# A planner's durations from the trace, values centred before the recurrence, subtractions moved to POOL, and a third lane in one hybrid layer

## The chip, the core and the metric

The kernel runs on one core of a Trainium2 chip. The metric is the device time of one execution in microseconds (us), as the median of three runs. TensorE is PE in what follows, its weight loads are PEld, VectorE is DVE, ScalarE is ACT, GpSimd is POOL and SyncE, which issues most DMAs, is SP.

## The reference

One layer of a diffusion backbone works on 1024 latent tokens behind 256 context tokens, with 1024 channels, all in float32. The parts that matter here:

```python
def wkv7_scan(r, decay, k, v, a, b, s0, reverse):
    # S_t = S_(t-1) diag(w_t) + (S_(t-1) a_t) b_t^T + v_t k_t^T ; y_t = S_t r_t
...
    for d in range(N_DIR):                       # forward and backward
        ys_c, s_ctx = wkv7_scan(*ins_c, s_zero, rev)
        ys_l, _ = wkv7_scan(*ins_l, s_ctx, rev)
        wkv_l = wkv_l + ys_l
        bonus_l = bonus_l + bon_l

def readout(wkv, bonus, gd):                     # per head of 64 channels
    mu = jnp.mean(wkv, -1, keepdims=True)
    var = jnp.mean(jnp.square(wkv - mu), -1, keepdims=True)
    yn = ((wkv - mu) * lax.rsqrt(var + LNX_EPS)).reshape(...)
    yn = yn * p['rwkv_lnx_g'] + p['rwkv_lnx_b']
    g = jax.nn.sigmoid(gd) @ p['rwkv_g_up']
    return ((yn + bonus.reshape(yn.shape)) * g) @ p['rwkv_w_out']
```

Around it stand an input projection, an S5 branch, gates, an output projection and a convolutional feed-forward network. The output of the recurrence is linear in `v`, so taking the mean over a head's 64 channels off `v` takes it off the output `wkv`; the bonus uses `v` with its mean.

## The kernel before

The kernel has three stages. **Stage A** makes the input projection and the S5 branch and writes the operands of the recurrence to DRAM. For each of the eight pairs of heads, `rw_job` leaves `xs` (the values), 80 PE transposes in all (L683) turn it by 128x128 pieces into PSUM tiles `pvt`, ACT copies them to `vt`, and DMAs store `vT_d`.

**Stage B** is the recurrence, for eight pairs of heads one after the other, 20 chunks of 64 tokens each. A *preparation* (`prep_nodes`) makes the operands of four chunks in one direction in a *lane* of buffers; there are two lanes, taken in turn. `inverse_nodes` inverts the small triangular blocks of up to eight chunks: DMAs L to LD to LN, 30 small DVE operations (L1073, L1076), DMAs TN to TD and TT to AD to AT, then small matmuls. `chain_nodes` is the recurrence itself, one step for each chunk: PE makes X, ACT copies X, PE makes U, DVE copies U (L1244), PE makes the new state, DVE writes S (L1267), and so on. `final_nodes` is the readout, in four blocks of 256 tokens a pair: loads of `y_d`, a DVE sum (L1336), a PE matmul by `E.center`, which takes the mean off (L1330), ACT scale and square, PE sums, 12 small DVE operations (L155 to L163), two spreads on PE, and more DVE work; it uses one buffer `fin`, and in the last pair three free blocks named `Q` as well. Beside all this runs the *filling*: gate and S5 matmuls that depend on nothing in the recurrence, 512 groups of three matmuls of 512 columns (L1464 to L1466). Their float32 operands are split in a high and a low half by `split`: SP loads `fr`, ACT makes the high half `fwh` or `fxh` (L1443), DVE subtracts it for the low half `fwl` or `fxl` (L1444).

The order of PE, ACT and DVE in stage B is written out by a *planner* (`Plan.order`). Each node has an engine, a cost in us and dependencies; the planner plays the engines through with these costs and emits the nodes in the order of its play. On PE a filling group is taken when little was issued lately or nothing else is ready. POOL and SP follow the emitted program through the framework's own scheduler.

**Stage C** holds the output projections and the feed-forward network; its first matmul (L202, `ygh`) needs `yg_d`, which the readout stores.

Of the kernel before, what the change touches and what calls it, by code (L numbers as in the profile page):

```python
# [12 lines left out]
AF = mybir.ActivationFunctionType  # L13
# [582 lines left out]
def stage_a(E):  # L596
    nc = E.nc
    with ExitStack() as st:
# [73 lines left out]
        for j in range(8):  # L672
# [48 lines left out]
class Node:  # L721

    __slots__ = ("eng", "cost", "deps", "succ", "emit", "due", "take", "give", "left", "ready", "bank", "cols", "fill", "tag", "key", "pri", "second")

    def __init__(self, eng, cost, deps, emit):
# [3 lines left out]
        self.cols, self.fill, self.tag, self.key, self.second = 0.0, None, None, False, None  # L729
# [7 lines left out]
class Plan:  # L737
# [19 lines left out]
    def order(self):  # L757
# [43 lines left out]
        def pick(h):  # L801

            skip, best = [], None
# [14 lines left out]
        while True:  # L818
# [8 lines left out]
            for e in heaps:  # L827
# [9 lines left out]
                if h or (e == "p" and fills):  # L837
# [6 lines left out]
                    else:  # L844
# [4 lines left out]
                        best = best or pick(h)  # L849
# [12 lines left out]
            n = best  # L862
            if n.eng == "p":
                hot.append((now, n.cols))
                total += n.cols
                left -= n.fill is None
# [6 lines left out]
            end = now + n.cost  # L873
# [30 lines left out]
def prep_nodes(E, g, c0, d, k):  # L904
# [37 lines left out]
    zn.cols = 2048  # L942
# [7 lines left out]
    for half in range(2):  # L950
# [6 lines left out]
        th.append(op("a", 0.36, [zn, ms], tanh, give=zs[half]))  # L957
    ts_ = op("v", 0.2, [th[0]], lambda: nc.vector.tensor_scalar(P[:, :, 1:65], P[:, :, 1:65], 0.5, 0.5, op0=OP.mult,
                                                                op1=OP.add))
    flat = P.rearrange("p c t -> p (c t)")  # L960
    scan = op("v", 0.34, [ts_], lambda: nc.vector.tensor_tensor_scan(flat, E.m65, flat, 0.0, op0=OP.mult, op1=OP.add))
    epi = op("a", 0.4, [scan], lambda: nc.scalar.activation(PI, P[:, :, 1:65], AF.Exp, scale=KAP,
                                                             bias=E.ln_half))
    ep = op("a", 0.31, [epi], lambda: nc.scalar.activation(P, P, AF.Exp, scale=-KAP))
    pc = op("g", 0.1, [ep], lambda: nc.gpsimd.tensor_copy(g.PC.tile[:, d, c0:c0 + nb], P[:, :, 64]))
    q = [op("v", 0.4, [ep, lkk], lambda: nc.vector.scalar_tensor_tensor(
        Q[:, :, 0:64], v3(o_(kk)), -1.0, P[:, :, 0:64], op0=OP.mult, op1=OP.mult))]
    t1 = op("v", 0.34, [th[1]] + q, lambda: nc.vector.scalar_tensor_tensor(kk, o_(ta), 1.0, kk, op0=OP.add,
                                                                           op1=OP.mult))
    tid = op("g", 0.54, [t1], lambda: nc.gpsimd.tensor_scalar(ta, ta, E.par("ka", j), E.ka2[:, j:j + 1], op0=OP.mult,  # L970
                                                              op1=OP.add))
    tk = op("v", 0.34, [tid, lkx], lambda: nc.vector.tensor_mul(ta, ta, o_(kx)))
    bk = [op("v", 0.4, [t1, epi], lambda: nc.vector.tensor_mul(BK[:, :, 0:64], v3(o_(kk)), PI))]
    bkk = op("v", 0.4, [tk, epi], lambda: nc.vector.tensor_mul(BK[:, :, 64:128], v3(ta), PI))
    rq = []
    if lat:
        rq = [op("v", 0.4, [ep, lr], lambda: nc.vector.tensor_mul(Q[:, :, 64:128], v3(o_(r)), P[:, :, 1:65]))]
        rkh = E.half[:, 32 + 8 * d + j:33 + 8 * d + j]
        bon = op("v", 0.4, [tk] + rq, lambda: nc.vector.scalar_tensor_tensor(r, o_(ta), rkh, r, op0=OP.mult,
                                                                              op1=OP.mult))  # L980
        g.done.append(op("g", 1.0, [bon], lambda: nc.gpsimd.dma_start(E.bon_d[j, d, :, bs], r)))
# [3 lines left out]
    for h in range(2):  # L985
        w = op("p", (0.5 if lat else 0.4), sc[-1:] or bk + [bkk] + q + rq, None, take=None if h else "F")
# [12 lines left out]
        w.emit, w.cols = mm, 8 * nn  # L999
# [13 lines left out]
    mq = [op("g", 1.2 if lat else 0.7, [cp], lambda: nc.gpsimd.tensor_mul(  # L1013
        A[:, :, 0:nn], A[:, :, 0:nn], E.mask[:, None, 0:nn].to_broadcast([128, 4, nn])))]
    tp = op("p", 0.35, bk + [bkk, blk.gate], None, take="F")
# [11 lines left out]
    tp.emit = tr  # L1027
# [882 lines left out]
```

## Time and profile before

| | |
|---|---|
| median of 3 runs | 3253.95 us (3245.26 to 3255.84) |
| profiled execution, its own time | 3263.26 us |
| span of the profile | 3261.5 us |
| mean granted PE clock | 0.913 of full |
| PE busy share of the span | 89% |
| DVE, ACT, POOL busy share | 56%, 42%, 14% |

The span is the time from the first to the last instruction; the execution's own time is 1.8 us longer, and 9.3 us above the median. A granted clock of 1.00 is 2.4 GHz, 0.50 is 1.2 GHz; a value between says that a stretch held both.

### The profile page before, as it was taken

What the parts mean: (1) busy time and instruction counts of PE and PEld (TensorE: products, weight loads), DVE (VectorE), ACT (ScalarE), POOL (GpSimd) and SP (SyncE); (2) the same over time, 40 slices, a digit from 0 to 9 for tenths busy, and PEclk for the clock granted to TensorE, in tenths of its full rate; (3) what the DMA queues carried; (4) which work ended last, traced back from release to release, by engine and by line L of the source; (5) the groups of instructions that cost most, each with busy time, mean ns of one, the idle gap of its engine ahead of it and who ended that gap; (6) DMA issues with size and microseconds to landing.
All of it is one profiled execution on the core that took longest, in us unless ns stands there. A gap on an engine that the chain in (4) does not pass through costs nothing.

```text
span 3261.5 us, 83856 instructions
## 1 busy us (share of the span) xinstructions
PE 2911.9 (89%) x34806; PEld 2197.0 (67%) x34806; DVE 1838.5 (56%) x4640; ACT 1371.0 (42%) x3055; POOL 471.7 (14%) x781
## 2 busy tenths in 40 slices
PE   6999887878579898999889888899998999999998
PEld 1788676767446666666666666666775888887876
DVE  7668777663345454668575667655534444344343
ACT  5224544435235454555444555442314433333332
POOL 0430011011222222223131222211000000000000
PEclk8999898989789888889788998889998999999999
DMA  5663333333465565455555455544531111113332
GB/s 190 207 168 104 128 117 125 110 119 120 145 167 148 152 161 135 120 135 133 130 143 126 119 141 146 125 125 139 193 120 55 52 48 49 46 52 112 107 107 74
DMA packets 556879, 399.32 MB, mean 122 GB/s; under 512 B 374225, under 2 KB 460497, under 8 KB 555217
## 3 DMA queue, kind: packets, MB, share of 16 engines
q1 hardware_dynamic: 517824, 300.96, 33.5%
q0 software_dynamic: 29312, 87.75, 8.0%
q10 hardware_dynamic: 9360, 5.25, 0.8%
q8 instruction: 273, 4.47, 0.6%
q14 instruction: 110, 0.89, 0.1%
HBM read 286.16 MB, written 112.85 MB: 122 GB/s over the span
## 4 chain that ended last, share of the span: by engine, by line
PE 61%; DMA 11%; issue 9%; DVE 9%; ACT 5%; SPq 3%; POOL 1%; ACTq 0%; DVEq 0%; POOLq 0%
PE pd L202 8%; PE pd L203 8%; PE pd L204 8%; PE bank L1464 5%; PE bank L1465 3%; PE bank L1466 3%; PE bank L1189 3%; PE bank L1184 3%; PE o L1751 3%; PE o L1752 3%; PE o L1753 2%; DMA wraw<-win 2%; PE bank L1330 1%; PE bank L994 1%; PE bank L947 1%
## 5 line engine op out<-in xcount | busy, mean ns | idle before, releaser
L189 DVE TENSOR_TENSOR wlo<-wraw,whi 128x512 fp32r<-128x512 f32 x276 | 184.0, 689 | 493.6 <-ACT whi L188 492.9
L188 ACT ACTIVATE whi<-wraw 128x512 fp32r<-128x512 f32 x276 | 165.8, 627 | 490.8 <-PE pd L203 243.4
L202 PE MATMUL pd<-hh,whi 128*128 128x512 f32 (+1 forms) x744 | 285.8, 384 | 51.8 <-ACT xs L624 35.2
L1464 PE MATMUL bank<-fxh,fwh 128*128 128x512 f32 x512 | 277.4, 542 | 12.1 <-ACT fo L1487 8.6
L202 PE MATMUL pd<-h2h,whi 128*128 128x512 f32 x704 | 275.5, 392 | 12.3 <-ACT h2h L1639 12.2
L204 PE MATMUL pd<-hh,wlo 128*128 128x512 f32 (+1 forms) x744 | 280.9, 378 | 1.5 <-DVE wlo L189 1.5
L203 PE MATMUL pd<-hl,whi 128*128 128x512 f32 (+1 forms) x744 | 282.1, 379 | 0.0
L204 PE MATMUL pd<-h2h,wlo 128*128 128x512 f32 x704 | 278.9, 397 | 0.0
L203 PE MATMUL pd<-h2l,whi 128*128 128x512 f32 x704 | 278.3, 396 | 0.3 <-DVE h2l L1640 0.2
L1465 PE MATMUL bank<-fxl,fwh 128*128 128x512 f32 x512 | 221.2, 432 | 0.5 <-issue 0.5
L1466 PE MATMUL bank<-fxh,fwl 128*128 128x512 f32 x512 | 220.8, 431 | 0.0
L202 PEld LDWEIGHTS pd<-hh,whi 128*128 128x128 f32 x744 | 148.3, 199 | 81.6 <-ACT xs L624 38.3
L204 PEld LDWEIGHTS pd<-hh,wlo 128*128 128x128 f32 x744 | 147.7, 199 | 25.8 <-DVE wlo L189 2.0
L203 PEld LDWEIGHTS pd<-hl,whi 128*128 128x128 f32 x744 | 148.4, 199 | 23.8 <-issue 2.5
L202 PEld LDWEIGHTS pd<-h2h,whi 128*128 128x128 f32 x704 | 133.2, 189 | 45.7 <-ACT h2h L1639 15.6
L203 PEld LDWEIGHTS pd<-h2l,whi 128*128 128x128 f32 x704 | 133.2, 189 | 33.0 <-DVE h2l L1640 2.1
L204 PEld LDWEIGHTS pd<-h2h,wlo 128*128 128x128 f32 x704 | 133.6, 190 | 26.6
L1464 PEld LDWEIGHTS bank<-fxh,fwh 128*128 128x128 f32 x512 | 104.3, 204 | 62.0 <-issue 20.0
L1444 DVE SCALAR_TENSOR_TENSOR fwl<-fr,fwh 128x512 fp32r<-128x512 f32 x128 | 92.6, 724 | 86.9 <-ACT fwh L1443 86.3
L1073 DVE TENSOR_TENSOR PR<-TN,LN 128x1 f32<-128x1 f32 (+9 forms) x360 | 118.5, 329 | 39.8 <-DMA LN<-LD 35.6
L1751 PE MATMUL o<-ph,whi 128*128 128x512 f32 x352 | 137.8, 396 | 2.2 <-ACT p L1725 2.2
L1752 PE MATMUL o<-pl,whi 128*128 128x512 f32 x352 | 138.9, 395 | 0.0
(395 smaller groups left out, 7209.3 us busy)
## 6 DMA issues: line engine op xcount, KB each, us to landing
wraw<-up SPq DMA_DIRECT2D x88, 256.0 KB
wraw<-down SPq DMA_DIRECT2D x88, 256.0 KB
wraw<-win SPq DMA_DIRECT2D x68, 256.0 KB
fin<-wmod SPq DMA_DIRECT2D x32, 512.0 KB
fr<-win SPq DMA_DIRECT2D x64, 256.0 KB
fr<-glu SPq DMA_DIRECT2D x64, 256.0 KB
s5U<-u_d SPq DMA_DIRECT2D x32, 320.0 KB
kk<-kk_d SPq DMA_DIRECT2D x80, 128.0 KB
```

The lines of the kernel that those rows point to most:

```text
L188: nc.scalar.activation(hi[:, c], raw, AF.Copy)
L189: nc.vector.tensor_sub(lo[:, c], raw, hi[:, c])
L202: nc.tensor.matmul(pt[:, :n], hi[:, c], xh, start=k == 0, stop=False)
L203: nc.tensor.matmul(pt[:, :n], hi[:, c], xl, start=False, stop=False)
L204: nc.tensor.matmul(pt[:, :n], lo[:, c], xh, start=False, stop=k == 7)
L1073: last = [op("v", 0.07 + k * k / 960.0, last, lambda lo=lo, hi=hi, k=k, s=s: nc.vector.tensor_tensor(out=PR[al, :k * k].rearrange("l (c m) ...
L1184: nc.tensor.matmul(out[OWN[e], d], w[OWN[e]], x[OWN[e]], skip_group_check=True, tile_position=(64 * e, 64 * e), **kw)
L1464: nc.tensor.matmul(o, hi[:, c], xh[:, k, :], start=k == 0, stop=False)
L1465: nc.tensor.matmul(o, hi[:, c], xl[:, k, :], start=False, stop=False)
L1466: nc.tensor.matmul(o, lo[:, c], xh[:, k, :], start=False, stop=k == 7)
L1751: nc.tensor.matmul(o, hi[:, c], ph, start=k == 0, stop=False)
L1752: nc.tensor.matmul(o, hi[:, c], pl, start=False, stop=False)
```

## The change

- The planner's costs are set to durations of the trace (the scan from 0.34 to 0.69 us, the readout's small operations from 0.07 to 0.2, chain matmuls from 0.35 to 0.23, and so on). A node carries a `mode`, the array shape of its matmuls: the planner adds 0.1 us where the shape changes, and prefers a node of the same shape within 0.5 us of due time. The counts of columns of two kinds of nodes change.
- The values are multiplied by `E.center` (identity minus the head's mean) in stage A, by 80 plain matmuls where 80 transposes stood. The 32 `center` matmuls of the readout and one ACT operation for each are gone; the scale joins a DVE operation.
- `split` subtracts on POOL where the scale is 1 (144 of 160 subtractions: the 128 weights and half of the 32 operands).
- Three lanes instead of two; the ring of value buffers `V` has two instead of three.

```diff
-                    nc.tensor.transpose(pv[:, q, :], xs[:, 128 * (i + q):128 * (i + q) + 128], E.ident)
+                    nc.tensor.matmul(pv[:, q, :], xs[:, 128 * (i + q):128 * (i + q) + 128], E.center, start=True, stop=True)
...
+            if mode is not None:
+                ok = [x for x in h if x[2].take is None or len(self.free[x[2].take]) > (x[2].second is not None)]
+                if not ok:
+                    return None
+                x = min(ok, key=lambda x: (x[0] + AFFINE * (x[2].mode != mode), x[1]))
...
-                        best = best or pick(h)
+                        best = best or pick(h, last)
...
+                shape, last = SWITCH * (n.mode != last), n.mode
...
-    scan = op("v", 0.34, [ts_], lambda: nc.vector.tensor_tensor_scan(flat, E.m65, flat, 0.0, op0=OP.mult, op1=OP.add))
+    scan = op("v", 0.69, [ts_], lambda: nc.vector.tensor_tensor_scan(flat, E.m65, flat, 0.0, op0=OP.mult, op1=OP.add))
...
-        pc = mm(E.center, Y, [a])
-        a = op("a", 0.27, [pc], lambda Y=Y, pc=pc: nc.scalar.activation(Y, E.ps(pc)[:, 0:256], AF.Copy, scale=E.par("lg", j)), give=pc)
-        q = op("a", 0.27, [pc], lambda y1=y1, pc=pc: nc.scalar.activation(y1, E.ps(pc)[:, 0:256], AF.Square), give=pc)
+        q = op("a", 0.38, [a], lambda Y=Y, y1=y1: nc.scalar.activation(y1, Y, AF.Square))
...
-LANES, PERIOD, SLACK, EVAC, STRETCH = 2, 120.0, 3.0, 0.0, 2.0
+LANES, PERIOD, SLACK, EVAC, STRETCH = 3, 120.0, 3.0, 0.0, 2.0
...
-        l = add("v", 0.6, [h], lambda: nc.vector.scalar_tensor_tensor(lo, r, scale, hi, op0=OP.mult, op1=OP.subtract))
+        if scale == 1.0:
+            l = add("g", 1.33, [h], lambda: nc.gpsimd.tensor_sub(lo, r, hi))
+        else:
+            l = add("v", 0.7, [h], lambda: nc.vector.scalar_tensor_tensor(lo, r, scale, hi, op0=OP.mult, op1=OP.subtract))
...
-        E.V = Ring(pl, [tile_(p, [128, 2, 4, 64], f"V{k}") for k in range(3)])
+        E.V = Ring(pl, [tile_(p, [128, 2, 4, 64], f"V{k}") for k in range(2)])
```

PE at the end of the recurrence, before (the last chain matmuls are those on `RB` and on `Q,S`; `fwh` and `fwl` are the filling):

```order
L1464 MATMUL bank_7321<-fxh,fwh_7431 128x512
L1465 MATMUL bank_7321<-fxl,fwh_7431 128x512
L1466 MATMUL bank_7321<-fxh,fwl_7434 128x512
L1330 MATMUL bank_7317<-fin_7422,center 128x256
L1184 MATMUL bank_7320<-RB_7417,U_7349 64x64 x4
L1184 MATMUL bank_7320<-Q_7415,S_7354 64x64 x4
L1330 MATMUL bank_7316<-fin_7422,bones 128x256
L1464 MATMUL bank_7321<-fxh,fwh_7429 128x512
L1465 MATMUL bank_7321<-fxl,fwh_7429 128x512
L1466 MATMUL bank_7321<-fxh,fwl_7432 128x512
L169 MATMUL bank_7315<-bones,fin_7422 128x2 x2
```

PE at the same place of the change (lines 1198 and 1203 are the chain, 1344 the readout, 1483 to 1485 the filling):

```order
L1485 MATMUL bank_7321<-fxh,fwl_7439 128x512
L1203 MATMUL bank_7320<-Q_7421,V_7393 64x64 x2
L1198 MATMUL bank_7319<-X_7348,TX_7341 64x64 x2
L1198 MATMUL bank_7320<-RB_7423,U_7349 64x64 x4
L1198 MATMUL bank_7320<-Q_7421,S_7354 64x64 x4
L169 MATMUL bank_7317<-bones,fin_7428 128x2 x2
L1344 MATMUL bank_7314<-fin_7428,bones 128x256
L176 MATMUL bank_7315<-ident,fin_7428 64x128 x4
L1344 MATMUL bank_7316<-fin_7428,gw_7429 128x256
L169 MATMUL bank_7317<-bones,Q_7403 128x2 x2
```

Before, 44 filling groups and six readout blocks stand behind the last chain matmul; in the change no filling group and five readout blocks do, and the `center` matmuls are gone.

POOL in the middle of stage B, before (L965 and L970 belong to a preparation, L1013 masks a block `Q`):

```order
L965 COPY PC_7359<-P_7373 128x4
L939 MEMSET P_7373 128x4
L970 TENSOR_SCALAR ta_7372<-ta_7372,par_t,ka_113 128x256
L1013 TENSOR_TENSOR Q_7397<-Q_7397,mask 128x4x64 x2
L1488 DMA sg_d<-fo_7436 1024x1x64
L1293 DMA y_d<-RB_7405 128x256 x2
L965 COPY PC_7359<-P_7366 128x4
```

And in the change (L1461 is the subtraction, L984 was L970, L1027 was L1013):

```order
L1461 TENSOR_TENSOR fwl_7438<-fr_7433,fwh_7435 128x512
L1027 TENSOR_TENSOR Q_7397<-Q_7397,mask 128x512
L1461 TENSOR_TENSOR fwl_7439<-fr_7434,fwh_7436 128x512
L1461 TENSOR_TENSOR fwl_7440<-fr_7432,fwh_7437 128x512
L979 COPY PC_7359<-P_7380 128x4
L953 MEMSET P_7380 128x4
L984 TENSOR_SCALAR ta_7379<-ta_7379,par_t,ka_113 128x256
L1027 TENSOR_TENSOR Q_7397<-Q_7397,mask 128x512
L1507 DMA sg_d<-fo_7442 1024x1x64
```

The subtractions stand between the masks and the preparations on POOL, in one queue with the stores of `y_d`, `sg_d` and `bon_d`.

## Rows read from the trace of the kernel before

**Rows 1.** The page, part 1: busy time, share of the span, instructions.

```profile
PE 2911.9 (89%) x34806; PEld 2197.0 (67%) x34806; DVE 1838.5 (56%) x4640; ACT 1371.0 (42%) x3055; POOL 471.7 (14%) x781
```

**Rows 2.** Windows: stretch, length, busy PE, PEld, DVE, ACT, POOL; clock, DMA share, GB/s.

```profile
640.00:885.00 245.00, 188.78 (x1149) 156.56 (x1148) 113.71 (x250) 100.51 (x168) 44.09 (x73) 0.87 0.44 136
920.00:2230.00 1310.00, 1178.78 (x25521) 829.31 (x25520) 804.68 (x2614) 639.98 (x1815) 313.43 (x499) 0.87 0.54 137
1000.00:1100.00 100.00, 92.97 (x2204) 64.30 (x2196) 58.78 (x184) 57.82 (x166) 27.41 (x44) 0.97 0.59 152
```

**Rows 3.** Windows of PE alone, around one stall: busy, granted clock.

```profile
1275.00:1280.00 5.00, 0.47 (x4) 0.66 0.69 105
1280.00:1285.00 5.00, 4.68 (x152) 0.50 0.80 261
...
1305.00:1310.00 5.00, 4.89 (x42) 0.50 0.35 101
1310.00:1315.00 5.00, 4.43 (x82) 0.93 0.33 46
```

**Rows 4.** Waits of PE, 920 to 2230: us in total, times, longest.

```profile
PE bank L1184 <- DVE U L1244: 21.3, 20, 3.2
PE bank L1330 <- DVE fin L1336: 19.1, 8, 6.4
PE bank L1109 <- DMA AT<-AD: 15.6, 14, 5.6
PE bank L1189 <- DVE S L1267: 10.0, 14, 3.6
```

**Rows 5.** Waits of SP's queue, 920 to 2230, same columns.

```profile
SPq L1442 <- DVE fwl L1444: 51.9, 16, 11.4
...
SPq L1442 <- DVE PR L1073: 34.3, 21, 6.2
```

**Rows 6.** Groups by line and form, 920 to 2230: busy, mean ns, idle before.

```profile
L1444 DVE SCALAR_TENSOR_TENSOR fwl<-fr,fwh 128x512 fp32r<-128x512 f32 x117 | 85.0, 728 | 79.3 <-ACT fwh L1443 78.8
...
L1013 POOL TENSOR_TENSOR Q<-Q,mask 128x512 f32<-128x512 f32 x62 | 82.0, 1328 | 71.6 <-ACT Q L1010 65.5 <-PE bank L1189 5.5
...
L961 DVE TENSOR_TENSOR_SCAN P<-m,P 128x260 f32<-128x260 f32 x76 | 52.8, 694 | 1.0
```

**Rows 7.** Line 683, whole run: duration min/median/max in ns.

```profile
L683 PE MATMUL pvt<-ident,xs x80: 272/273/477, 323.5 to 870.8; 128*128 128x128 f32 x80
```

**Rows 8.** Line 543, plain float32 matmuls of the same size, 64 instructions.

```profile
L543 PE MATMUL s5py<-s5U,s5M x128: 270/275/552, 295.6 to 785.9; 128*128 128x128 f32 x128
```

**Rows 9.** Timeline of PE: a `center` matmul between filling matmuls.

```profile
2247.40 0.59 PE L1330 MATMUL bank<-Q,center 128*128 128x256 f32 x2
...
2248.06 0.40 PE L1465 MATMUL bank<-fxl,fwh 128*128 128x512 f32 x1
```

**Rows 10.** Timeline: POOL and DVE at 1590 us.

```profile
1590.43 1.29 POOL L1013 TENSOR_TENSOR Q<-Q,mask 128x512 f32<-128x512 f32 x1
1590.50 1.25 DVE L161 SCALAR_TENSOR_TENSOR fin<-fin 128x4 f32<-128x4 f32 x1
```

**Rows 11.** Line 161, 920 to 2230: duration min/median/max in ns.

```profile
L161 DVE SCALAR_TENSOR_TENSOR fin<-fin x78: 147/161/1252, 1344.5 to 2218.3; 128x4 f32<-128x4 f32 x78
```

**Rows 12.** Timeline of PE and POOL from the recurrence's end to stage C.

```profile
2230.26 0.22 PE L1184 MATMUL bank<-Q,S 64*64 64x64 f32 x2
...
2261.66 0.54 POOL L1356 DMA_DIRECT2D yg_d<-fin  x1 [2.03 <-DVE fin L1354]
2276.90 0.54 POOL L1356 DMA_DIRECT2D yg_d<-fin  x1 [10.22 <-DVE fin L1354]
2278.89 0.39 PE L1464 MATMUL bank<-fxh,fwh 128*128 128x512 f32 x1
2279.57 0.39 PE L1464 MATMUL bank<-fxh,fwh 128*128 128x512 f32 x1
2287.19 0.80 PE L202 MATMUL pd<-ygh,whi 128*128 128x512 f32 x1 [6.77 <-ACT whi L188]
```

More of the change, by code (lines that the diff above doesn't have):

```diff
@@ L721 @@
 class Node:
-    __slots__ = ("eng", "cost", "deps", "succ", "emit", "due", "take", "give", "left", "ready", "bank", "cols", "fill", "tag", "key", "pri", "second")
+    __slots__ = ("eng", "cost", "deps", "succ", "emit", "due", "take", "give", "left", "ready", "bank", "cols", "fill", "tag", "key", "pri", "second", "mode")
     def __init__(self, eng, cost, deps, emit):
@@ L728, in __init__ @@
         self.succ, self.due, self.take, self.give, self.ready = [], 1e9, None, None, 0.0
-        self.cols, self.fill, self.tag, self.key, self.second = 0.0, None, None, False, None
+        self.cols, self.fill, self.tag, self.key, self.second, self.mode = 0.0, None, None, False, None, 128
 LAG = {"p": 0.27, "a": 0.22, "v": 0.22, "g": 0.25, "s": 2.2, None: 0.0}
@@ L799, in arrive, with pick @@
             heapq.heappush(wait[n.eng], (n.ready, seq[id(n)], n))
-        def pick(h):
+        last = 128
+        def pick(h, mode=None):
+            if mode is not None:
[3 more added lines that the diff above has]
+                x = min(ok, key=lambda x: (x[0] + AFFINE * (x[2].mode != mode), x[1]))
+                h.remove(x)
+                heapq.heapify(h)
+                return x[2]
             skip, best = [], None
@@ L862, in order @@
             n = best
+            shape = 0.0
             if n.eng == "p":
+                shape, last = SWITCH * (n.mode != last), n.mode
                 hot.append((now, n.cols))
@@ L872, in order @@
                 n.cost *= COLD
-            end = now + n.cost
+            end = now + n.cost + shape
             if n.eng == "p":
@@ L941, in prep_nodes @@
     zn = op("p", 0.44, gates, None, take="F")
-    zn.cols = 2048
+    zn.cols, zn.mode = 1024, 96
     zs = (zn, pl.second(zn))
@@ L998, in mm @@
                                      stop=True, tile_position=(64 * e, 64 - 64 * e))
-        w.emit, w.cols = mm, 8 * nn
+        w.emit, w.cols, w.mode = mm, 8 * nn, 64
     first = sc[0]
@@ L1240, in g2 @@
                 own(pU, d, tx[:, d, si, :], X.tile[:, d], start=end and d == 0, stop=True)
-        gu.emit, gu.cols = g2, 512
+        gu.emit, gu.cols, gu.mode = g2, 512, 64
         X.users.append(gu)
@@ L1292, in step @@
                 for d in HALF:
-                    g.done.append(op("g", 1.0, B.out, lambda d=d: nc.gpsimd.dma_start(
+                    g.done.append(op("g", 0.55, B.out, lambda d=d: nc.gpsimd.dma_start(
                         E.y_d[j, d, :, 64 * (i - 7):64 * (i - 3)], RB[:, d].rearrange("p c t -> p (c t)"))))
@@ L1458, in dense @@
                 k = 4 * half + q
-                n = add("p", 0.65, x[k] + parts, None, take=None if first else "D")
+                n = add("p", FILL, x[k] + parts, None, take=None if first else "D")
                 first = first or n
@@ L1486, in evac @@
                 out = E.sg_d[i, :, t0:t0 + 512]
-            n = add("a", 0.48, [last, g], lambda: nc.scalar.activation(dst, src(), AF.Tanh, scale=0.5), give=first)
-            o.users = [add("g", 1.0, [n], lambda: nc.gpsimd.dma_start(out, mem))]
+            n = add("a", 0.78, [last, g], lambda: nc.scalar.activation(dst, src(), AF.Tanh, scale=0.5), give=first)
+            o.users = [add("g", 0.6, [n], lambda: nc.gpsimd.dma_start(out, mem))]
             written[i, t0] = o.users[0]
@@ L1496, in evac_b @@
             sb, g = outs.next()
-            n = add("a", 0.48, [last, g], lambda: nc.scalar.activation(sb.tile, E.ps(first), AF.Tanh), give=first)
+            n = add("a", 0.6, [last, g], lambda: nc.scalar.activation(sb.tile, E.ps(first), AF.Tanh), give=first)
             hold[0] = sb, n
```

108 lines of the change are left out of this document (56 added, 52 removed).

## The prediction

> **What bounds the kernel now.** I read the busy shares first: PE is busy 89% of the span, DVE 56%, ACT 42%, POOL 14% [rows 1]. Then I read the windows, because these shares mix three stages. The recurrence fills 920 to 2230, and there PE is busy 1178.8 of 1310 us, DVE 804.7, ACT 640.0, POOL 313.4 [rows 2]. The reader is to see that PE is the bound there, yet falls short in two ways. It stands idle for 1310 - 1178.8 = 131 us, and its mean granted clock is 0.87. With levels of 1.0 and 0.5 that is 26% of the time at half rate, and half of that time, about 170 us, is lost where PE streams. So 301 us of the 1310 are no work at full clock.
>
> The two losses hang together. At 1275 PE does almost nothing for 5 us; the granted clock falls to 0.50 and is back at 0.93 only in the slice that begins at 1310 [rows 3]. A stall of some 5 us so costs some 15 us more. The stretch 1000 to 1100 shows what the same code does without such stalls: PE busy 93.0%, clock 0.97 [rows 2], a loss of 7 + 3 = 10 us in 100 in place of 23.
>
> Third, the waits of PE. Of its 131 us idle, 21.3 wait for DVE's copy of U, 19.1 for the readout's first DVE sum L1336, 10.0 for DVE's S, 15.6 for the DMA AT<-AD of the inversion [rows 4]; what is left is spread over ACT and many small causes. SP's queue, finally, waits 51.9 us in L1442 for a DVE subtraction that has not yet freed a buffer, and 34.3 us in the same line behind L1073 [rows 5]. SP issues in order, so the loads of the inversion and the readout stand behind that wait. Late DVE work is thus the largest single cause, directly and through SP.
>
> **The change, part by part.**
>
> *Centre matmuls, -14.* The readout loses 32 `center` matmuls. From the start of one, 2247.40, to the second matmul of the next filling group, 2248.06, are 0.66 us [rows 9]; a filling matmul alone takes a third of the 0.68 us between two groups' starts, 0.23 [rows 12]. A `center` so costs 0.43, 32 of them 14 us of PE. The stall of 19.1 before it does not go with it: the next matmul on PE (L169 on the squares) needs the same loads. It only can shrink, which the last item holds.
>
> *Transposes to matmuls, +8.* In stage A 80 transposes, one record each of 0.273 [rows 7], become plain float32 matmuls, for which such a matmul of the same size shows two records of 0.275 [rows 8]. At the most that is 80 x 0.275 = 22 us, at the least nothing, since PE is busy only 188.8 of 245 us where most of them lie [rows 2]. I take 8: PE is nearer to full than to free there.
>
> *Filling moved into the recurrence, +30; a shorter tail, -15.* In the order of before 44 filling groups stand behind the last chain matmul, in the change none. At 0.68 each [rows 12] that is 30 us of PE work that now has to be done before the chain ends. The tail that they leave, 2230.3 to 2287.2, is 56.9 us. It does not go away: the readout's loads, sums and stores take their time with nothing to hide behind. In the change five readout blocks follow instead of six, so the fifth, whose store in before was issued at 2261.7, is the last. From the last store at 2276.9 to stage C's first matmul took 10.3 [rows 12]. So 2261.7 - 2230.3 + 10.3 = 41.7, 15 less than 56.9.
>
> *Subtractions on POOL, +12.* 144 subtractions of 0.728 leave DVE [rows 6]: 105 us, 8% of the stretch. On POOL nothing like them is in the trace; the nearest row is the two-input mask L1013 of the same 128x512 at 1.328 [rows 6]. That gives 191 us, so POOL would be busy 504 of 1310: hidden as a sum. The price is elsewhere. A DVE operation of 128x4, L161, takes 0.161 in the median but 1.252 at worst [rows 11], and one such case began inside a POOL mask and ended with it [rows 10]. So the mask holds DVE out. If half of the 144 meet a DVE operation and hold it for half their length, 144 x 0.5 x 0.66 = 48 us are added to DVE, less than the 105 taken off. DVE has idle time for it; I let a quarter, 12, reach PE. Bounds: 0, if no subtraction meets the chain, and 48, if all of it does.
> The Trainium skill says it more broadly (GPSIMD Engine Reference, Specifications): POOL's SBUF interfaces are shared with VectorE, which contends when an instruction has two SBUF inputs or a two-port mode. By it any of the 144 could take its full 1.33 from DVE, 191 us against 105 taken off. The one case in rows 10 agrees, the median in rows 11 says that it is rare; it is the third rival below.
>
> *Third lane, value ring of two: 0.* A preparation is more ahead, so PE finds one more kind of work. A value buffer serves a block of four steps, some 4 x 1310 / 160 = 33 us; with two, the next one's loads can be issued when the block before last is done, a block ahead of need. If SP is held there all the same, the loads behind it are late, which the last item's lower bound holds.
>
> *The durations, -100.* The planner's play had DVE too fast: its cost for the scan was 0.34, the trace says 0.694 [rows 6], and the small readout operations stood at 0.07 against 0.161 [rows 11]. Chain matmuls it had too slow (0.35, now 0.23). So PE came to the chain's matmuls before DVE had written U and S; that is what rows 4 show. The four waits above are 66 of 131 us, half. With true durations and 105 us less DVE work I let two thirds of that half go, and the clock with it in proportion: 301 x 0.5 x 0.67 = 100. Bounds: 0, if the play was not the cause, and 189, if all of the stretch ran as 1000 to 1100 did (1310 - 301 = 1009 of work; 1009 / 0.9 = 1121).
>
> That the shapes now cost the planner something is worth nothing here: counted in both orders, PE changes the array shape 1341 times in stage B before and 1386 times in the change. The preference does not do what it is for.
>
> **Sum.** -14 + 8 + 30 - 15 + 12 - 100 = -79. Against the profiled execution of 3263.3 this is 3184; the median of the runs is 9.3 lower, so 3254 - 79 = 3175.
>
> **The rivals.**
>
> *Stalls all but gone.* If the recurrence runs like its best stretch, the last item is -189 in place of -100, and the sum is -168: 3086. For it: POOL takes what SP waited for, and a stall avoided saves three times itself [rows 3]. Against it: AT<-AD and the readout's loads hang on DMA, whose lag in the planner is unchanged.
>
> *The change does not do what it says.* If PE's waits come from how the engines drift from any play, true durations change nothing. Then the last item is 0 and the rest stays, +21: 3275, slower. For it: the moved filling has to be paid and POOL is a new in-order queue whose subtractions stand behind waits for others. Against it: the waits in rows 4 are on the engine whose costs were furthest off.
>
> *POOL holds DVE.* If each subtraction holds DVE for the full 1.33, DVE gains 191 - 105 = 86 us of work; the chain's copies of U and S stand behind it in DVE's queue, the durations are wrong again, and no stall goes. With half of the 86 on PE, 43 in place of 12, and no recovery: 3254 + 21 + 31 = 3306. It decides from the point where a subtraction holds DVE longer than the 0.73 that it takes off. For it: rows 10. Against it: the median of rows 11, and POOL's mask has run 62 times in this stretch beside a DVE busy 61%.
>
> **How the numbers follow.** My forecast holds with a chance of 0.46, its own range 3120 to 3225. The first rival has 0.27 (3060 to 3120), the second 0.14 (3240 to 3300), the third 0.06 (3290 to 3330); 0.07 is left for a small gain, 3225 to 3250. Forecast, first rival and most of the small gain are faster by over 0.3%, which is 10 us and about what a measurement of this kernel can tell from no change: 0.77. Within 0.3% lie the rest of the small gain and the near end of the second rival: 0.09. Slower: 0.14. The range 3060 to 3262 leaves out the third rival and most of the second.
>
> **What would show it.** In the profile after, between the first chain step and the last: PE's waits for U, S and the readout's first sum below 25 us together (50.4 now), a mean clock of 0.91 or more, PE idle below 95 us. SP's waits for `fr` should be short, or be for POOL. In the tail no filling matmul, and some 42 us from the last chain matmul to stage C. DVE's small operations should still have a median near 0.16; a mean above 0.4 would show the third rival. Stage A should end within 10 us of where it did. I am wrong if the clock stays at 0.87 with the waits only moved to other lines, or if DVE's two-input operations grow beside POOL's subtractions.

## The result and the profile after

The change is slower by about half a per cent: 3264.99 us in the median of 20 runs (3251.08 to 3284.94) against 3250.53 for the kernel before in 20 runs, a ratio of 1.0055 with a 95% interval of 1.0036 to 1.0075. I had forecast 3175. What came is close to the second rival, "the change does not do what it says" (3275), but by two errors that cancel, as the section on the prediction shows.

The profiled execution of the change spans 3265.7 us, that of before 3261.5. The one of before ran 12.8 us over its median (3263.3 against 3250.5), so the two profiles lie closer together (4.5 us) than the medians do (14.5), and what is read from them below accounts for the smaller difference. Line numbers in the changed kernel are larger by 1 in stage A, by 14 in stage B up to the readout and by up to 19 behind it.

Page of the change, part 1, to lay beside [rows 1]:

```profile
PE 2913.4 (89%) x34822; PEld 2200.2 (67%) x34822; DVE 1817.6 (56%) x4496; ACT 1361.7 (42%) x3023; POOL 655.1 (20%) x925
```

144 subtractions left DVE, yet DVE's busy time fell by 20.9 us only. That is taken up with e2.

Windows of the change, columns as in [rows 2]: the two stretches of [rows 2], then the chain from its first copy of U to its last, then the tail to stage C's first matmul.

```profile
920.00:2230.00 1310.00, 1168.27 (x25279) 820.81 (x25279) 792.31 (x2474) 635.52 (x1783) 491.27 (x637) 0.88 0.56 142
1000.00:1100.00 100.00, 98.53 (x2170) 65.67 (x2173) 45.50 (x139) 56.94 (x159) 36.45 (x47) 0.96 0.61 153
1015.40:2255.50 1240.10, 1118.45 (x24575) 791.91 (x24575) 747.08 (x2386) 604.77 (x1722) 452.88 (x592) 0.89 0.55 138
2255.50:2293.90 38.40, 20.67 (x97) 13.14 (x97) 20.74 (x99) 5.07 (x10) 4.30 (x8) 0.58 0.39 132
```

The same two stretches, chain and tail, in the kernel before:

```profile
979.00:2229.20 1250.20, 1124.81 (x24652) 796.46 (x24643) 769.00 (x2508) 612.73 (x1753) 296.92 (x475) 0.87 0.54 136
2229.20:2287.20 58.00, 48.06 (x259) 36.22 (x257) 33.97 (x130) 14.50 (x29) 5.95 (x11) 0.97 0.47 153
```

Three things are to be seen. The chain starts 36.4 us later (1015.4 against 979.0). It is 10.1 shorter, but not because PE stands still less: 1240.1 - 1118.5 = 122 us of it are idle, before 125. And the tail is 19.6 shorter, as 44 filling groups have left it. So stage C begins 36.4 - 10.1 - 19.6 = 6.7 us later.

Waits of PE in the change, 920 to 2230, to lay beside [rows 4]:

```profile
PE bank L1389 <- DMA fin<-wmod: 29.1, 6, 15.0
PE bank L1123 <- DMA AT<-AD: 25.2, 26, 4.8
PE bank L1198 <- DVE U L1258: 16.7, 19, 2.5
PE bank L1203 <- DVE S L1281: 10.5, 10, 1.9
...
PE bank L1344 <- ACT fin L1351: 5.1, 2, 2.8
PE bank L1344 <- DVE fin L1352: 5.0, 2, 2.8
```

The wait for the readout's first sum has gone with the `center` matmul; waits of 5.1 us for the readout's squares (L1351) and 5.0 for its sum of the bonus (L1352) are left in its place. U and S still hold PE for 27.2 us (31.3 before), and what the readout gave back is taken by two DMA waits: AT<-AD (15.6 before) and fin<-wmod, of which 10.1 lie in the chain (5.0 before) and 19.0 ahead of it, where the kernel before waits 14.9.

Waits of SP's queue in the same stretch, to lay beside [rows 5], and then SP's queue as stage B starts (start, length, operation):

```profile
SPq L1458 <- POOL fwl L1461: 102.9, 46, 9.8
```

```profile
907.60 15.48 SPq L1458 DMA_DIRECT2D fr<-xn_d  x1
...
938.64 2.10 SPq L1079 DMA_DIRECT2D LD<-L  x4
```

SP waited 51.9 us in this line for DVE's subtraction; now it waits 102.9 for POOL's. All waits in the line together went from 158.5 to 144.4, so they changed their names more than their size. At 907.6 one load of the filling's operand holds the queue for 15.5 us, and LD<-L of the inversion is issued at 939; in the kernel before it was issued at 915.8. It would be wrong to put that hold down to POOL. The same stretch in the kernel before, and then in e2, the change with its subtractions back on DVE:

```profile
890.35 14.60 SPq L1367 DMA_DIRECT2D fin<-wmod  x1
```

```profile
895.25 15.79 SPq L950 DMA_DIRECT2D kx<-k_d  x2
```

In all 18 kernels of this study SP's queue shows such a stretch of 14.3 to 16.5 us, straight behind the last vT_d<-vT_d of stage A, whatever is issued there.

The late start has two parts. The value matmuls of stage A, to lay beside [rows 7], give one: the last one began at 870.8, now at 889.0.

```profile
L684 PE MATMUL pvt<-center,xs x160: 270/275/579, 324.6 to 889.0; 128*128 128x128 f32 x160
```

The other 18.2 us lie between that matmul and the first U. Windows of this stretch, before and in the change:

```profile
870.80:979.00 108.20, 66.47 (x1060) 40.67 (x1062) 49.50 (x131) 41.95 (x95) 25.51 (x36) 0.75 0.64 170
```

```profile
889.00:1015.40 126.40, 83.95 (x1317) 52.54 (x1316) 65.30 (x148) 49.24 (x113) 57.35 (x66) 0.74 0.66 172
```

PE is busy 17.5 us longer there and idle as long as before (42 us): work of the preparations now stands ahead of the chain (316 matmuls on `Q,BK` against 208), and the chain has fewer of them (2240 against 2304).

### The profile page after: what moved, and what is told of

It is laid out like the page before. It is cut to its first block, busy times and chain, and to the rows that moved or that the text cites. A ratio compares the mean times of both kernels' runs of the same rounds, so it can differ in the third digit from the quotient of the medians.

```text
span 3265.7 us, 83787 instructions
## 1 busy us (share of the span) xinstructions
PE 2913.4 (89%) x34822; PEld 2200.2 (67%) x34822; DVE 1817.6 (56%) x4496; ACT 1361.7 (42%) x3023; POOL 655.1 (20%) x925
## 4 chain that ended last, share of the span: by engine, by line
PE 64%; DMA 12%; issue 8%; DVE 7%; ACT 4%; SPq 3%; POOL 1%; ACTq 0%; DVEq 0%; POOLq 0%
PE pd L202 9%; PE pd L204 8%; PE pd L203 8%; PE bank L1483 5%; DMA wraw<-win 3%; PE bank L1485 3%; PE bank L1484 3%; PE bank L1203 3%; PE o L1770 3%; PE o L1771 2%; PE o L1772 2%; PE bank L1198 2%; PE bank L1008 1%; PE bank L961 1%; DVE PR L1087 1%
## 5 line engine op out<-in xcount | busy, mean ns | idle before, releaser
L1461 POOL TENSOR_TENSOR fwl<-fr,fwh 128x512 fp32r<-128x512 f32 x128 | 169.8, 1327 | 218.5 <-ACT fwh L1459 217.9
L1087 DVE TENSOR_TENSOR PR<-TN,LN 128x1 f32<-128x1 f32 (+9 forms) x360 | 141.2, 392 | 57.5 <-DMA LN<-LD 54.1
L202 PEld LDWEIGHTS pd<-h2h,whi 128*128 128x128 f32 x704 | 133.7, 190 | 40.2 <-ACT h2h L1658 13.7
```

The costliest lines, as they stand in the source:

```text
L202: nc.tensor.matmul(pt[:, :n], hi[:, c], xh, start=k == 0, stop=False)
L1087: last = [op("v", 0.14 + k * k / 520.0, last, lambda lo=lo, hi=hi, k=k, s=s: nc.vector.tensor_tensor(out=PR[al, :k * k].rearrange("l (c m) ...
L1461: l = add("g", 1.33, [h], lambda: nc.gpsimd.tensor_sub(lo, r, hi))
```

## The experiments

The runs were taken in four rounds on four chips, each with the kernel before on the same chip; the ratios to it, with 95% intervals, are compared across rounds. The positions and idle times are from one profiled execution of each kernel. From each trace I read the chain (first to last copy of U), PE's idle time in it, the readout blocks stored behind the last copy of U, and the tail from there to stage C's first matmul. The theories are named by letters: D, the new durations cost; B, they cost by pushing readout blocks behind the chain; S, the start; L, the third lane; H, POOL holding DVE.

| kernel | ratio | first U | chain | idle in it | blocks behind | tail |
|---|---|---|---|---|---|---|
| before | 1 | 979 | 1250 | 125 (10.0%) | 6 | 58 |
| the change | 1.0055 [1.0036, 1.0075] | 1015 | 1240 | 122 (9.8%) | 5 | 38 |
| e1 centring alone | 0.9986 [0.9956, 1.0016] | 993 | 1242 | 119 (9.5%) | 5 | 37 |
| e2 change, low halves on DVE | 1.0146 [1.0102, 1.0191] | 999 | 1243 | 136 (11.0%) | 8 | 77 |
| e3 change, two lanes | 1.0088 [1.0057, 1.0119] | 995 | 1262 | 138 (10.9%) | 5 | 40 |
| e4 durations alone | 1.0269 [1.0232, 1.0306] | 986 | 1217 | 126 (10.3%) | 13 | 153 |
| e5 change, old table | 1.0082 [1.0053, 1.0111] | 996 | 1210 | 127 (10.5%) | 7 | 76 |
| e6 centring and POOL | 0.9951 [0.9924, 0.9977] | 995 | 1229 | 122 (10.0%) | 4 | 43 |
| e7 change, no shape costs | 1.0186 [1.0153, 1.0218] | 1006 | 1186 | 122 (10.3%) | 12 | 128 |
| e8 e4 with two readout buffers | 1.0040 [1.0011, 1.0070] | 999 | 1215 | 126 (10.3%) | 4 | 62 |
| e9 change, shape price only | 1.0111 [1.0080, 1.0143] | 1008 | 1266 | 131 (10.4%) | 6 | 44 |
| e10 e6 with two value buffers | 0.9977 [0.9953, 1.0001] | 998 | 1223 | 117 (9.5%) | 4 | 47 |
| e11 e3, two readout buffers | 1.0108 [1.0071, 1.0144] | 1001 | 1250 | 129 (10.3%) | 4 | 38 |
| e12 e10, two readout buffers | 1.0027 [0.9999, 1.0056] | 1001 | 1204 | 132 (11.0%) | 4 | 63 |
| e13 chain's durations alone | 1.0099 [1.0066, 1.0132] | 979 | 1202 | 118 (9.8%) | 12 | 136 |
| e14 e6, lag +0.08 | 1.0139 [1.0103, 1.0175] | 1003 | 1283 | 131 (10.2%) | 5 | 40 |
| e15 e6, lag +0.18 | 1.0111 [1.0073, 1.0148] | 992 | 1272 | 144 (11.4%) | 4 | 35 |
| e16 change, no shapes, two lanes, two readout buffers | 1.0046 [1.0019, 1.0072] | 1008 | 1245 | 126 (10.1%) | 4 | 39 |

### One part at a time

**e1, centring alone**, on the kernel before (old table, two lanes):

```diff
-                    nc.tensor.transpose(pv[:, q, :], xs[...], E.ident)
+                    nc.tensor.matmul(pv[:, q, :], xs[...], E.center, start=True, stop=True)
...
-        pc = mm(E.center, Y, [a])
```

> The kernel before with the centring moved and nothing else (80 centring matmuls in stage A, none in the readout). In the change the first copy of U stands at 1015 us against 979, and the last matmul of the value transposes in stage A at 889 against 871. Theory S (the loss lies ahead of the chain, and its part in stage A is the longer centring matmuls): stage A's last value matmul comes 10 to 18 us later, the chain is 14 us shorter, ratio 0.998 to 1.003. Theory D (the new durations are what costs): stage A is as before, only the 14 us go, ratio 0.996. Theory L (the third lane's preparations crowd stage A's end): as D, 0.996.

0.9986, no difference that can be told. The last value matmul came at 881.4 instead of 870.8, the first U 13.7 later, and chain and tail together went from 1308 to 1279. Theory S holds for stage A and for the ratio; the chain is 8 us shorter, not 14. Chain and tail of the whole change are 1240 + 38 = 1278: what else the change holds took nothing off there.

**e2, the low halves back on DVE**, in the change:

```diff
-        if scale == 1.0:
-            l = add("g", 1.33, [h], lambda: nc.gpsimd.tensor_sub(lo, r, hi))
-        else:
+        if True:
             l = add("v", 0.7, [h], ...)
```

> The change with all subtractions of the low halves back on DVE, at 0.7 in the planner. Theory S (at the start of stage B SP is held for 15 us by a load that waits for POOL's subtraction of an earlier tile): first copy of U at about 995 instead of 1015, ratio 0.999. Theory D and theory L: first copy of U stays near 1015, ratio 1.005. Theory H (POOL's subtractions hold DVE in the chain): first to last copy of U 20 to 30 us shorter than the 1240 of the change, ratio 0.995 to 0.998, and DVE's L1087 back from 392 to about 330 ns.

1.0146: without POOL the change is worse by 0.9%. The start is earlier, near what theory S said (999), though its ratio of 0.999 is missed, as eight blocks stand behind the chain and the tail is 77 us. Theory H falls as to the time: the chain is as long as in the change (1243). Its mechanism is there all the same. Page part 1 of this kernel, then of e1 and of e6, which is e1 with the subtractions on POOL:

```profile
PE 2902.6 (88%) x34822; PEld 2192.5 (67%) x34822; DVE 1837.1 (56%) x4640; ACT 1357.4 (41%) x3023; POOL 472.2 (14%) x781
```

```profile
PE 2906.5 (90%) x34822; PEld 2200.5 (68%) x34822; DVE 1834.1 (56%) x4640; ACT 1361.3 (42%) x3023; POOL 473.7 (15%) x781
```

```profile
PE 2896.6 (89%) x34822; PEld 2195.3 (68%) x34822; DVE 1823.5 (56%) x4496; ACT 1362.0 (42%) x3023; POOL 654.8 (20%) x925
```

From e2 to the change DVE's busy time falls by 1837.1 - 1817.6 = 19.5 us, from e1 to e6 by 10.6, while 105 us of subtractions [rows 6] left it. Its other operations have grown by 85 to 94 us, 0.59 to 0.65 for each of the 144 subtractions. Which ones grew can be read from the inversion's small operations, here in e2 and then in the change. L1087 reads two SBUF tiles, L1090 one:

```profile
L1087 DVE TENSOR_TENSOR PR<-TN,LN 128x1 f32<-128x1 f32 (+9 forms) x360 | 111.7, 310 | 68.0 <-DMA LN<-LD 64.7
L1090 DVE TENSOR_REDUCE TN<-PR 128x1 f32<-128x1 f32 (+9 forms) x360 | 83.2, 231 | 3.1
```

```profile
L1087 DVE TENSOR_TENSOR PR<-TN,LN 128x1 f32<-128x1 f32 (+9 forms) x360 | 141.2, 392 | 57.5 <-DMA LN<-LD 54.1
L1090 DVE TENSOR_REDUCE TN<-PR 128x1 f32<-128x1 f32 (+9 forms) x360 | 83.1, 231 | 3.8
```

With the subtractions on POOL the mean of L1087 is 392 ns, without them 310, as theory H said (about 330); L1090 does not move. From e1 to e6 the same two lines go from 333 to 403 and stay at 232.

**e3, two lanes and three value buffers**, in the change:

```diff
-LANES, PERIOD, SLACK, EVAC, STRETCH = 3, 120.0, 3.0, 0.0, 2.0
+LANES, PERIOD, SLACK, EVAC, STRETCH = 2, 120.0, 3.0, 0.0, 2.0
-        E.V = Ring(pl, [tile_(p, [128, 2, 4, 64], f"V{k}") for k in range(2)])
+        E.V = Ring(pl, [tile_(p, [128, 2, 4, 64], f"V{k}") for k in range(3)])
```

> The change with two preparation lanes and three value buffers as before. Theory L: the last value matmul of stage A comes back from 889 to about 875 us, the first copy of U to about 997, ratio 0.999 to 1.001. Theories S, D and H: nothing moves by more than 5 us, ratio 1.005; a chain that is longer by 10 us or more would show that the lane helps there, ratio 1.008 or more.

1.0088. The start is 20 us earlier as theory L said, but the chain is 22 longer: a shift, no gain. The interval overlaps that of the change.

**e4, the durations alone**: the change without moved centring, subtractions on POOL, third lane and smaller value ring, and with both constants for shapes at 0. The changed column counts stay in; they were not timed apart. Of the table, for instance:

```diff
-        gx = op("p", 0.35, state + B.q[0] + B.q[1] + kt + first, None)
+        gx = op("p", 0.23, state + B.q[0] + B.q[1] + kt + first, None)
...
-            r = op("v", 0.07, [r] if i else [r, pv], f, **({} if i else {"give": pv}))
+            r = op("v", 0.2, [r] if i else [r, pv], f, **({} if i else {"give": pv}))
```

> The kernel before with the new durations in the planner and nothing else. Theory D (the durations repair no stall, and the filling that they move into the chain is paid there): first to last copy of U as long as before or longer (1250 us or more), ratio 1.000 to 1.006. Theory S (the durations do help in the chain, and the start loses it again): 1240 us or less with 30 us of filling more in it, no late start, ratio 0.990 to 0.994. My prediction's term would give 0.97 to 0.98.

1.0269, the largest effect of all, and in the wrong direction. Windows of this kernel, chain and tail:

```profile
986.20:2203.40 1217.20, 1091.37 (x24505) 781.92 (x24497) 736.01 (x2381) 608.77 (x1737) 284.32 (x460) 0.88 0.53 134
2203.40:2356.40 153.00, 70.92 (x302) 47.35 (x302) 57.56 (x236) 13.78 (x33) 9.18 (x17) 0.60 0.26 86
```

The chain is 33 us shorter than before, and PE is busy 33 us less in it: no stall is repaired. Idle are 125.8 us, as before, and PE's waits for U and S in the chain are 13.0 and 14.7, together 27.7 against 31.3. What the chain has lost is found behind it. Timeline of their stores on POOL in the tail (start, length, operation, idle before):

```profile
2264.76 0.54 POOL L1371 DMA_DIRECT2D yg_d<-fin  x1 [13.22 <-DVE fin L1369]
2278.59 0.54 POOL L1371 DMA_DIRECT2D yg_d<-fin  x1 [13.28 <-DVE fin L1369]
2292.30 0.54 POOL L1371 DMA_DIRECT2D yg_d<-fin  x1 [13.17 <-DVE fin L1369]
```

Waits of PE in the tail, 2203 to 2357:

```profile
PE bank L1344 <- DVE fin L1350: 50.1, 8, 7.9
PE bank L176 <- DVE fin L163: 19.5, 8, 2.4
```

Window of the same kernel over six of these blocks:

```profile
2256.20:2338.00 81.80, 32.05 (x108) 19.92 (x108) 26.31 (x107) 4.48 (x12) 3.24 (x6) 0.50 0.23 72
```

Thirteen blocks, instead of six, are left when the chain ends. Most of them go one after the other through the single `fin` buffer, one each 13.7 us. For each PE waits 50.1 / 8 = 6.3 us for the loads and the first sum; it is busy 32 of the 82 us of the window, and the granted clock is 0.50, its lower level, throughout.

### What pushes the blocks out

**e5, the change with the old table**, and **e6**, the same with two lanes and three value buffers. Both are the kernel before with centring moved and this:

```diff
-        l = add("v", 0.6, [h], lambda: nc.vector.scalar_tensor_tensor(lo, r, scale, hi, ...))
+        if scale == 1.0:
+            l = add("g", 1.33, [h], lambda: nc.gpsimd.tensor_sub(lo, r, hi))
+        else:
+            l = add("v", 0.6, [h], lambda: nc.vector.scalar_tensor_tensor(lo, r, scale, hi, ...))
```

> The change without its durations, column counts and array shapes in the planner (the old table; only the subtraction on POOL stands there at 1.33): centring moved, low halves on POOL, three lanes, two value buffers. Durations alone cost 2.7% and left 13 readout blocks behind the last U copy instead of 6. Theory B (the new durations harm by pushing readouts behind the chain, and the rest of the change is good by itself): 5 or 6 blocks behind the chain, ratio 0.985 to 0.993. Rival theory R (POOL's relief is only worth something against the backlog that the durations make): ratio 0.997 to 1.002, as centring alone.

> As the run before it, but with two lanes and three value buffers: the kernel before with centring moved and low halves on POOL. Theory B: the third lane is worth little, ratio within 0.004 of the run with three lanes. Theory L (the third lane delays the start): first U copy 15 us or more earlier than with three lanes, and the ratio lower by 0.004 or more.

e6 is at 0.9951 the fastest kernel of this study, faster than the kernel before and than the change. e5 at 1.0082, with 7 blocks behind the chain, missed the numbers of both its theories. The difference of the two is the lane with the smaller value ring. Theory L for e6 has the ratio right and the reason wrong: the first U comes at 995 as against 996, and what e6 has less is behind the chain, 4 blocks and a tail of 43 instead of 7 and 76. Chain and tail account for some 14 us; the medians lie 39 apart (e5 was profiled 11 us below its median, e6 11 above), so most of that difference is not explained by the profiles.

**e7, the change without shape costs**, and **e9, with the price alone**:

```diff
-SWITCH, AFFINE = 0.1, 0.5
+SWITCH, AFFINE = 0.0, 0.0
```

```diff
-SWITCH, AFFINE = 0.1, 0.5
+SWITCH, AFFINE = 0.1, 0.0
```

> The change with the costs of a change of array shape set to nothing (both constants 0), durations kept. Theory B: the shapes are neither the gain nor the loss, ratio 1.002 to 1.009 as the change, PE idle in the chain 115 to 130 us. Theory A (the shapes' preference is what moves readouts and fillings): ratio off from 1.0055 by 0.006 or more in either direction, with another number of readout blocks than 5 behind the chain.

> The change with the planner's preference for the same array shape set to 0, its price of 0.1 for a change of shape kept. With both at 0 the ratio was 1.0186 and 12 readout blocks stood behind the last U copy, in the change 5. Theory T (the price only makes PE slower in the play, by 0.1 for each of some 1400 changes, so the chain is planned longer and more readouts are placed inside it): about 6 blocks behind, ratio 1.002 to 1.009, as the change. Theory A (the preference keeps shapes together and PE gains by that): ratio 1.013 to 1.020.

Without both, 12 blocks stand behind the chain, the tail is 128 us and the ratio 1.0186. So theory A's bound for e7 is met, and theory B's ratio missed. With the price alone (e9) 6 blocks are left and the ratio is 1.0111, between what theories T and A gave; the rest, 0.0056, comes with the preference. Theory T explains the blocks and more than half of the time, not all; what the preference does for the rest is not shown.

**e8, e4 with a second readout buffer**, which also takes two value buffers instead of three and one `g_up` tile for both:

```diff
-NBLK, NRAW, NW, NOUT, NFIN = 5, 3, 3, 3, 1
+NBLK, NRAW, NW, NOUT, NFIN = 5, 3, 3, 3, 2
```

> Durations alone, with a second readout buffer of 6 x 256 (paid for by two value buffers instead of three; both readout buffers share the one g_up tile). Durations alone gave 13 blocks behind the chain, each 13.7 us on the one buffer, a tail of 153 us. Theory B: with two buffers the blocks overlap and fewer are left, tail below 80 us, ratio 1.000 to 1.010. Theory P (the blocks are late because the planner's order places their work late on the engines, whatever the buffers): 10 or more blocks behind the chain, though they may overlap there; tail 90 us or more, ratio 1.012 or more.

1.0040 instead of 1.0269, with 4 blocks behind and a tail of 62 us. Theory B is met, theory P falls: nearly all of the loss of the durations is the backlog on one buffer. Windows, chain and tail:

```profile
999.00:2213.00 1214.00, 1088.46 (x24427) 783.83 (x24425) 735.93 (x2507) 602.87 (x1733) 288.22 (x465) 0.86 0.52 133
...
2213.10:2274.60 61.50, 54.81 (x274) 42.58 (x274) 28.73 (x100) 16.17 (x30) 5.38 (x10) 0.99 0.42 141
```

PE is now busy 55 of the 62 us of the tail, at full clock, and idle in the chain for 125.5 us as ever.

**e10, two value buffers** in e6, **e11, two readout buffers** in e3 and **e12** in e10 (the edits are those shown above):

> Centring moved and low halves on POOL, two lanes, old table, but two value buffers in place of three. With three buffers and two lanes this was 0.9951, with two buffers and three lanes 1.0082. Theory V (the second value buffer less is what costs): 1.004 to 1.010, with longer waits of SP in the loads of vT. Theory L (the third lane costs): 0.993 to 0.998.

> The change with two readout buffers, two lanes instead of three to pay for them (both readout buffers share one g_up tile). With two lanes and one buffer it was 1.0088 with 5 blocks behind the chain. Theory B (a second buffer helps only by the blocks that it keeps from standing behind the chain): 4 blocks behind instead of 5, ratio 1.000 to 1.008. Theory Q (the second buffer saves PE's waits in the chain as well): ratio below 0.998 and PE idle in the chain below 110 us.

> Centring moved, low halves on POOL, old table, two lanes, two value buffers and two readout buffers. Theory B: 4 blocks stand behind the chain with one buffer already, so nothing is to be had: within 0.005 of the run with two value buffers and one readout buffer. Theory Q: 0.980 to 0.988.

The ring costs 0.3% (0.9951 to 0.9977, the intervals overlap; from the last value matmul to the first U 121.5 us against 110.7 in e6), the lane the other 1% of e5. For e10 theory L holds and theory V falls. Where few blocks stand behind the chain, a second buffer brings nothing: 1.0108 after 1.0088, 1.0027 after 0.9977, both with overlapping intervals. e11 so missed the ratios of both its theories, theory Q also the idle time, and e12 lies at the edge of what theory B gave. PE then waits 16 and 23 us for gw<-g_up, the tile that both buffers share.

### Whether PE's stalls answer to the planner

**e13, only the chain's durations**, on the kernel before (PE groups 0.35 to 0.23, copies 0.30 to 0.28, updates 0.25 to 0.28, the others that the expectation names, and the issue of `y_d` on POOL from 1.0 to 0.55):

> The kernel before with the new durations of the chain's own operations alone (its PE groups 0.35 to 0.23, readout 0.6 to 0.44, copies 0.30 to 0.28, the scaled state 0.24 to 0.34, updates 0.25 to 0.28). Theory B (a chain that is shorter in the play has less room for readouts): 12 readout blocks behind the last U copy, a tail over 100 us, ratio 1.012 to 1.025. Rival W (the waits for U and S are of the chain's own costs, and true ones cure them): PE's waits for U and S below 15 us together, ratio below 1.0.

Twelve blocks, a tail of 136, 1.0099 (a little under what theory B gave). U and S hold PE for 23.2 us instead of 31.3, but PE idles 118 us. Rival W falls.

**e14 and e15**, e6 with more lag between engines in the play:

```diff
-LX, LS = 0.02, 1.5
+LX, LS = 0.1, 1.5
```

> Centring moved and low halves on POOL, two lanes, old table (0.9951 as it was), with 0.08 more lag between two engines in the play. Theory N (the engines drift; no table changes PE's idle share): idle 9 to 11% of the chain, waits for U and S 25 to 40 us, ratio 0.990 to 1.002. Theory W (PE's waits answer to what the play believes of the hand-overs): waits for U and S below 18 us, idle below 8%, ratio below 0.988.

> As the run before it, with 0.18 more lag. Theory N: idle as before, chain longer by the filling that it takes in (none is left behind it), ratio 0.992 to 1.005. Theory W: waits for U and S below 10 us, ratio below 0.985.

Both are slower (1.0139, 1.0111), outside the ratios of either theory. Idle are 131 and 144 us, the waits for U and S 36.8 and 41.8, as theory N said, and no filling is left behind the chain; theory W falls. To tell the planner of later hand-overs does not shorten them.

**e16**, the change without shape costs, with two lanes, two value buffers and two readout buffers:

> Everything of the change but the shapes' price and the third lane, with two readout buffers (and two value buffers). 4 blocks stand behind the chain. Durations with two readout buffers were 1.004; centring took 0.0014, POOL between 0.0035 and 0.009. Theory B (the parts add up once the backlog is gone): ratio 0.992 to 1.000. If the durations cured stalls, PE idle in the chain would be below 8% and the ratio below 0.988.

1.0046: with the backlog gone the new table is no better than the old one with the same parts (e12, 1.0027, the intervals overlap), and worse than e10 with one readout buffer (0.9977). Theory B's sum was too good: the parts do not add up.

## Why the prediction was wrong

**The durations, -100: this step failed.** I read PE's waits for U, S and the readout as lateness that the old durations had caused, and let two thirds of them go. Of the 66 us so counted, 15.6 waited for a DMA and 19.1 for a sum behind loads, whose lag in the planner, as I wrote myself, was unchanged. In e4, where nothing else of the change but the column counts was in, PE's idle time in the chain was 125.8 us against 125.4. Over the 18 profiled kernels, with several tables, two or three lanes and three lags, it lay between 117 and 144 us, 9.5 to 11.4% of the chain, while the names of the waits moved from one to another (U from 10 to 30 us, AT<-AD from 0.2 to 25). My second rival had this outcome, true durations that change nothing in PE's waits; its reason, that the engines drift from any play, is not shown by it. The durations changed something that I had not costed: which work stands inside the chain. With chain matmuls at 0.23 instead of 0.35 fewer readouts are placed between its steps (e13: 12 blocks behind it with the chain's own durations alone), and each that is left to the single buffer costs 13.7 us. What sets the 10% is not settled; no run here moved it below 9.5%.

**Where the 86 us lie.** Forecast was -79; in the profiles stage C began 6.7 later. For chain and tail together I had -14 + 30 - 15 + 12 - 100 = -87, and they lost 29.7, so 57 are missing there. The start was to be 8 later and was 36.4, which are the other 28. With the durations at 0 the same terms give the second rival's +21, +13 for chain and tail and +8 for the start. Chain and tail came out 43 better than that, the start 28 worse. That 3275 lies so near to 3265 is luck.

**The clock.** The mean granted clock of the chain went from 0.87 to 0.89, not to the 0.91 that I had asked for; e1 shows 0.89 with the old table. "Clock in proportion" so had nothing to be in proportion to.

**The shapes, worth nothing: wrong.** Without them the change is 1.3% slower (e7). I had counted the changes of shape in the order, not what the price does to the play: with the price alone 6 blocks instead of 12 stand behind the chain (e9).

**POOL, +12: wrong in sign, though the hold was under-, not overestimated.** I gave 48 us of DVE at most; it was 85 to 94. DVE's two-input operations grew beside the subtractions, which I had named as a sign of being wrong. The 0.59 to 0.65 that a subtraction holds stays under the 0.73 from which my third rival decides, and on POOL the kernel is faster: e2 to the change by 0.9%, e1 to e6 by 0.35%, the last with overlapping intervals. The 0.9% is the tail, 77 to 38, less a start that is 16 later. For the 0.35% I have no shown cause. The rule that I weighed there (the Trainium skill, GPSIMD Engine Reference, Specifications: contention with two SBUF inputs) is borne out by these sums, at half of an instruction's length on the mean, and by L1087 with two SBUF inputs growing from 310 to 392 ns where L1090 with one stays at 231.

**The third lane and the value ring, 0: off.** With the old table the lane costs 1.0% (e10 to e5) and the ring 0.3%; with the new one both together gain 0.3% (e3 to the change, with overlapping intervals). So the same lane costs with one table and not with the other; e5 has 7 blocks behind the chain where e10 has 4. How the lane brings that about was not tested.

**Right in mechanism and size:** the tail was 41.7 forecast and 38.4 measured, with no filling left in it and five blocks. Stage A's +8 came out at 10.6 in e1 and 18.2 in the change, within the bound of 22, but past the 10 that I had named as a sign. Over the 14 kernels with moved centring the last value matmul came 3.5 to 18.2 us later, 10.4 on the mean, over the three others without it within 1.4 us of the kernel before. The subtraction's 1.328 [rows 6] was measured on POOL as estimated:

```profile
L1461 POOL TENSOR_TENSOR fwl<-fr,fwh 128x512 fp32r<-128x512 f32 x127 | 168.5, 1328 | 211.9 <-ACT fwh L1459 211.3
```

**The moved filling, +30, is not seen as a cost.** The chain took in 43 groups more (477, before 434), 29 us at my price, and yet PE's busy time in it fell by 6.3. In e1 the chain took in 28 groups, 19 us at that price; with the `center` term and the shorter tail my terms give -14 - 15 + 19 = -10 for chain and tail, and they lost 29. One reason is to be seen in the change: some of the preparations' work had moved ahead of the first U. The granted clock of 0.89 instead of 0.87 may be another; the shares were not taken apart.

**The late start** I had costed only in stage A: it is 36 us, of which 18 in stage A and 18 between the last value matmul and the first U. The second part is work, not waiting: PE is idle 41.6 to 47.9 us there in all 18 kernels, and by and large the stretch is longer where PE has more to do in it. With POOL's subtractions gone (e2) it is 119.2 instead of 126.4, with two lanes (e3) 118.2, but from e1 to e6 POOL adds nothing to it (111.3, 110.7), and e10, which differs from e6 in the value ring alone, has 10.8 more. Which part of the change brings the work forward stays open.

## What to carry to other kernels

A planner with truer durations need not give a faster program. Here it did not touch the bound engine's idle share at all, and it moved side work with a long, serial path through one buffer behind the main chain, where nothing hides it. Before costing such a change, count in both orders what stands behind the last step of the chain and price it by its serial period, not by its engine time; and before putting a share of the idle time down to a cause, ask whether any earlier order of the same kernel had less. Parts of a change that go through a planner need not add up, so time them apart: here two of them, centring and POOL, are together faster than the kernel before and than the whole change.

## What the runs showed of the hardware

A POOL subtraction of two 128x512 SBUF tiles, 1.33 us long, cost DVE's other work 0.59 to 0.65 us on the mean, so that moving 105 us off DVE lowered its busy time by only 10.6 to 19.5 us. In the inversion it was the operation with two SBUF inputs that grew: L1087 went from a mean of 310 ns to 392, while L1090, with one input, stayed at 231 (e2 and the change). The chain's copy of U out of PSUM, L1258, did not grow either (289 and 288), which fits a chain as long in the one as in the other. DVE's smallest readout operation does not show it: L161 has its rare long cases with the subtractions on DVE too, up to 1230 ns in e2 and 1209 in the change, with a median of 155 and 158.
